# A two-layer decoder trunk on one core: Norm's matrix 64 bytes later, three short products, and eight more unread products at the start

## The chip, the core and the metric

The kernel runs on 1 core of one Trainium2 chip. A core has five engines, each with a queue of its own: TensorE (PE in the profile; its weight loads are listed apart as PEld and overlap the products), VectorE (DVE), ScalarE (ACT), GpSimd (POOL) and SyncE (SP, which issues DMAs here). DMAs move data between HBM and the on-chip memory. TensorE's results go to banks of a separate small memory, eight of 128 x 512 numbers here. The metric is the device time of one execution in microseconds (us). The time before is the median of 3 runs; the profile and the trace come from one more execution.

## What is computed

Two layers on a sequence of 512 tokens with 1024 features, float32. Each layer has a token mixer and a feed-forward part. Both get a root-mean-square norm of their input, scaled and shifted by values worked out from a vector `c`, and both are added to the residual stream through a gate. Cut to what matters:

```python
c_act = jax.nn.silu(c)
for i in range(2):
    mod = c_act @ ada_w[i] + ada_b[i]           # six vectors: shift, scale, gate, twice
    h = rmsnorm(x, norm_tok_g[i]) * (1.0 + sc_t) + sh_t
    y = retention_mixer(h, ...) if i == 0 else mlstm_mixer(h, ...)
    x = x + gt_t * y
    h = rmsnorm(x, norm_ffn_g[i]) * (1.0 + sc_f) + sh_f
    x = x + gt_f * conv_ffn(h, ...)
return rmsnorm(x, final_g)
```

`rmsnorm(x, g)` is `x * rsqrt(mean(x*x) + 1e-6) * g` over the features. Both mixers have four heads, with query and key projections of 256 columns and values and gates of 512 columns a head. Retention turns queries and keys by position (rope), the mLSTM sends them through a short causal convolution. The feed-forward part has 2 x 2816 inner features, a convolution over three tokens, and `silu(a) * b`.

## The kernel before, in words

**Arithmetic.** Every large product is made of three products of a faster format (float32r): a matrix is split into a high part `hi` and a low part `lo`, and `hi*hi + hi*lo + lo*hi` is summed (`mm3`). ScalarE makes high parts (`whi` for weights; `hh`, `t24h`, `t3h`, `yh`, `ggh` for activations), VectorE or ScalarE with an adding DMA the low ones (`wlo`, `hl` and so on). Activations lie with features on the 128 partitions and tokens along the row, so most products take a 128 x 128 weight block as the stationary matrix and 256 or 512 tokens as the moving one. Where the profile says "p<-hh,whi", the output bank is `p`, and `hh` and `whi` are what it reads.

**Folding.** Most projections are made in a Strassen-like scheme: two pairs of weight tiles (`wa`, `wb`) and sums of them (`ws`, `wt`) give seven products of 256 columns in place of eight. `seven` (line 824) lists the seven steps of one fold in the order 1, 2, 6, 5, 7, 4, 3 as items; `PairStream.product` (line 789 on) issues the twelve TensorE products of a step. A fold uses two banks, with the parts `c11`, `c12`, `c21`, `c22`. `c22` is first written by VectorE in the step for product 7. `fold_pairs` (line 853) makes two folds one after the other: for a head's query and key (`ret_q`, line 1754, `ml_q`, line 1896), or for its gates. The feed-forward part has 19 such folds a layer in `folded` (line 870), a unit of 84 products each, with the products that lead back to the residual stream ("po") among them.

**Stages.** In order of time: the opening with retention head 0 (`ret_start`, line 1604); retention heads 1 to 3, woven together by `heads` (line 1357): q, v and g are the projections, s the scores, a the attention, o the output projection; a boundary; the feed-forward part 0; a boundary; mLSTM heads 0 to 3, again by `heads`; a boundary; the feed-forward part 1; and the last boundary with the final norm. `heads` calls `q(2)` after head 0's output projection. mLSTM's `q(0)` comes after the value projection of `v_items` (line 1011), whose products have 512 columns.

**Boundaries.** `boundary` (line 1070) runs the last output blocks in two halves of the tokens ("po", 256 columns). In between, the norm's root for the first half is made: `SquareSum.root` (line 697) sums the squares over the partitions by two products "pms" with the matrix `ones_d`, filled with 1/1024, as stationary operand; the root for the second half is made in the same way during the first projection of the next part ("pf", `Start.rest`, line 1188). All weight tiles of a boundary and of its "pf" products start at column `OFF` = 16 (64 bytes) of their buffers, as do the folds' tiles. Plain projections ("pp", "po" with 512 columns) start at column 0. In the feed-forward part the class `Beside` (line 530) places the low part of every fourth block at 64 bytes off.

**Short products.** At the start of each boundary and of each feed-forward part's folds there is already a product of 16 columns ahead of the first real one (lines 913 and 1046). It reads the same weights and activations as the first product, and nobody reads its result:

```python
def short_product(o, w, b):
    PE.matmul(o, w, b, start=True, stop=True, skip_group_check=True)
```

**The opening.** `ret_start` adds up the squares of `x` on ScalarE and VectorE, makes the means over the partitions with `means` (line 1642: products "pms" that read one column of `ones_d` as the moving operand), the root, and a copy of it across partitions by four products with the identity `eye`. Meanwhile the modulation vectors come from VectorE's products with 512 KB tiles `ada`. Then eight rounds `products(k)` (line 1648) of 24 products each ("pst" and "pc") follow, each as soon as `h0[k]` is there (`hh` from ScalarE, `hl` from VectorE). Unread products keep TensorE at work in between: `busy(n)` (line 1616) issues n products of 512 columns of ones, 6, 1 and 1 times by the constant `BUSY`.

**Order.** All instructions are first collected by the class `Plan`, which keeps its own estimate of each one's time (`occ`) and due time, places them by due time on five queues with a model of buffers and transfers, and then issues them in that order; the order on each engine is fixed from there on. A product's estimated time feeds the due times of all that follows. On-chip buffers come from fixed pools: 62 slots of 512 columns, 18 wide tiles of 1024 + 64 columns (4352 bytes), and a pool of constants that is laid out one after the other, with `ones_d`, `ones_v` (1/512) and `ones_1` near its start:

```python
for name, v in (("d", 1.0 / D), ("v", 1.0 / DV), ("1", 1.0)):
    o = fixed(const, [P, P], F32R, f"ones_{name}")
    V.memset(o[:].bitcast(F32), v)
    ones[name] = o
```

Since every recorded instruction is issued by one helper, nearly all rows of the profile carry that helper's line, L386; groups are told apart by the tiles' names.

Of the kernel before, what the change touches and what calls it, by code (L numbers as in the profile page):

```python
# [16 lines left out]
P = 128  # L17
# [35 lines left out]
ROPE_DUE = 200.0  # L53
BUSY = (6, 1, 1)
ALIVE = (0, 0, 256, 256, 256, 256, 0, 0)
SUMMED = 6
# [333 lines left out]
def trunk(ctx: ExitStack, tc: tile.TileContext, xT, cb, pos, vec, ident, decay, zmask, ada, w_s0, w_in0, w_v0,  # L390
# [45 lines left out]
    for name, v in (("d", 1.0 / D), ("v", 1.0 / DV), ("1", 1.0)):  # L436
        o = fixed(const, [P, P], F32R, f"ones_{name}")
        V.memset(o[:].bitcast(F32), v)
        ones[name] = o
# [222 lines left out]
    def short_product(o, w, b):  # L662


        PE.matmul(o, w, b, start=True, stop=True, skip_group_check=True)

# [156 lines left out]

    def seven(use, streams, done, between=lambda j: None):

# [3 lines left out]
        def mk(n):  # L829
            def fn(w):  # L830
                if n == ORDER[0]:
                    for s in streams:
                        s.open(w[0])
                        fs.append(slot("fs"))
                for s, f in zip(streams, fs):
                    o = {1: s.c21, 2: s.c11, 5: s.c12, 3: s.c12}.get(n, s.c21)
# [15 lines left out]

    def fold_pairs(srcs, terms, thens, between=lambda j: None):

# [5 lines left out]
        for n, (src, then) in enumerate(zip(srcs, thens)):  # L860
            seven(FoldUse(src, n), [PairStream(terms, then)], each(then), lambda j: between(7 * n + j))

# [741 lines left out]
    def ret_start():  # L1604
# [10 lines left out]

        def busy(n, w=T):

            for _ in range(n):
                PE.matmul(pss[0][:, :w], ones["1"][:], warm[:, :w], start=True, stop=True, skip_group_check=True)

# [64 lines left out]
        for m in range(1, KT):  # L1685
            square(m)
            if m != SUMMED:
                add(m - 1, m)
            else:
                means(m - 1, True)  # L1690
            alive(m, ALIVE[m])
# [10 lines left out]
        gemv(0, 0, mod[0])  # L1702
        busy(BUSY[1])
        for t in range(4):
            PE.matmul(ps[:, t * P : t * P + P], rc[:, t : t + 1].broadcast_to([P, P]), eye[:, :P], start=True,
                      stop=True, skip_group_check=True)
        busy(BUSY[2])
        xr = xrs[0] = slot("xr")
# [45 lines left out]
    def ret_q(i, between=nothing):  # L1754
        thens = [half_pair(R[i], name, rope) for name in ("q", "k")]
        if i:
            fold_pairs(pair_srcs(w_in0, i * 8), sums0.terms, thens, between)
            return
# [304 lines left out]
```

## Time and profile before

| | |
|---|---|
| median of 3 runs | 1486.17 us (1485.03 to 1488.53) |
| the profiled execution's own time | 1483.02 us |
| its span | 1481.2 us |
| mean granted TensorE clock | 0.995 |
| TensorE busy | 1460.8 us (99%), 10550 products |
| VectorE busy | 1292.4 us (87%) |
| ScalarE busy | 1064.9 us (72%) |
| GpSimd busy | 267.1 us (18%) |
| DMA traffic | 306.16 MB, mean 207 GB/s |

The profile is one execution. The span goes from the first to the last instruction. A product's busy time in the profile is longer than the distance between two products, since they are pipelined: a product of 256 columns is listed with some 278 ns, while the next one starts some 115 ns later. So the pace of a stretch is read from starts: the stretch's length over the number of products that start in it. "Idle before, releaser" names the engine and tile whose end let an instruction start. The clock is the share of its full speed that TensorE was granted.

### The profile page before, as it was taken

How to read it: one execution, taken by the hardware profiler on the slowest of the kernel's cores; microseconds unless marked ns; L12 is line 12 of the kernel's file. 1: busy time of each engine (PE TensorE's matmuls, PEld its weight loads, DVE VectorE, ACT ScalarE, POOL GpSimd, SP SyncE). 2: the span in 40 equal slices, each digit the busy share in tenths (PEclk: the TensorE clock that was granted, in tenths of full speed). 3: DMA queues.
4: the chain of work that ended last, by engine and by line, in shares of the span. 5: the costliest groups of instructions: out<-in, count | busy, mean ns of one | idle time of the engine just before them, and what ended most of it. 6: DMA issues, size and time to landing. Idle time of an engine off the chain costs nothing. (4 is left out here: it accounts for less than half of the span.)

```text
span 1481.2 us, 27389 instructions
## 1 busy us (share of the span) xinstructions
PE 1460.8 (99%) x10550; PEld 1372.3 (93%) x10550; DVE 1292.4 (87%) x2167; ACT 1064.9 (72%) x1604; POOL 267.1 (18%) x295
## 2 busy tenths in 40 slices
PE   8999999999999999999999999999999999999998
PEld 6899999998999999999999998999989999999997
DVE  7899979787989889898897999999989988877866
ACT  5578758776588667676678985989856777667663
POOL 0334223222011111011001321222121011111010
PEclk8999999999999999999999999999999999999999
DMA  9878989887588999899567876878877678668661
GB/s 361 252 178 199 286 212 246 226 249 198 158 222 199 263 268 247 220 241 247 156 182 166 206 207 184 198 192 200 253 192 187 163 181 210 154 170 209 165 162 58
DMA packets 90821, 306.16 MB, mean 207 GB/s; under 512 B 11953, under 2 KB 14513, under 8 KB 90690
## 3 DMA queue, kind: packets, MB, share of 16 engines
q1 hardware_dynamic: 60882, 197.18, 38.8%
q0 software_dynamic: 29520, 106.97, 38.6%
q8 instruction: 82, 1.34, 0.4%
q14 instruction: 49, 0.40, 0.1%
q10 hardware_dynamic: 288, 0.27, 0.1%
HBM read 195.29 MB, written 2.12 MB: 133 GB/s over the span
## 5 line engine op out<-in xcount | busy, mean ns | idle before, releaser
L386 PE MATMUL p<-hh,whi 128*128 128x256 f32 x1026 | 284.3, 278 | 2.5 <-DVE p L386 2.5
L386 PE MATMUL p<-hl,whi 128*128 128x256 f32 x1024 | 283.5, 277 | 0.0
L386 PE MATMUL p<-hh,wlo 128*128 128x256 f32 x1024 | 281.2, 277 | 0.0
L386 ACT ACTIVATE wlo<-whi 128x1024 fp32r<-128x1024 f32 (+1 forms) x205 | 215.4, 1055 | 26.3 <-PE po L386 15.6
L386 PEld LDWEIGHTS p<-hh,whi 128*128 128x128 f32 x1026 | 193.0, 188 | 3.7 <-DVE p L386 3.1
L386 PEld LDWEIGHTS p<-hl,whi 128*128 128x128 f32 x1024 | 192.8, 188 | 0.5
L386 PEld LDWEIGHTS p<-hh,wlo 128*128 128x128 f32 x1024 | 191.3, 188 | 0.0
L386 PE MATMUL p<-t24h,whi 128*128 128x256 f32 x768 | 170.1, 278 | 3.3 <-DVE p L386 2.2
L386 PE MATMUL po<-ggl,whi 128*128 128x512 f32 (+1 forms) x448 | 152.8, 343 | 0.0
L386 PE MATMUL po<-ggh,whi 128*128 128x512 f32 (+1 forms) x448 | 151.9, 344 | 0.5 <-ACT whi L386 0.5
L386 PE MATMUL po<-ggh,wlo 128*128 128x512 f32 (+1 forms) x448 | 152.3, 343 | 0.0
L386 PE MATMUL p<-t24l,whi 128*128 128x256 f32 x512 | 142.0, 277 | 0.0
L386 DVE SCALAR_TENSOR_TENSOR x<-po,mod,x 128x512 f32<-128x512 f32 (+1 forms) x184 | 113.5, 628 | 30.6 <-PE po L386 29.8
L386 ACT CAST whi<-raw 128x1024 fp32r<-128x1024 f32 (+1 forms) x113 | 113.7, 1017 | 35.2 <-DMA raw<-w_s 9.2
L386 PEld LDWEIGHTS p<-t24h,whi 128*128 128x128 f32 x768 | 130.3, 188 | 5.8 <-DVE p L386 3.1
L386 DVE SCALAR_TENSOR_TENSOR cv<-p,vecs,cv 128x511 f32<-128x511 f32 (+1 forms) x152 | 111.2, 743 | 12.5 <-ACT cv L386 12.2
L386 DVE SCALAR_TENSOR_TENSOR ada<-ada,c_ext 128x1025 f32<-128x1025 f32 x96 | 119.6, 1247 | 0.6 <-DMA ada<-ada 0.6
L386 PE MATMUL po<-yl,whi 128*128 128x256 f32 (+1 forms) x352 | 115.6, 329 | 0.0
L386 PE MATMUL po<-yh,whi 128*128 128x256 f32 (+1 forms) x354 | 115.6, 329 | 0.0
L386 PE MATMUL po<-yh,wlo 128*128 128x256 f32 (+1 forms) x352 | 115.6, 329 | 0.0
L386 POOL DMA_DIRECT2D wlo<-wa x55 | 47.6, 866 | 353.6 <-ACT wlo L386 168.7
L386 ACT CAST whi<-ws 128x1024 fp32r<-128x1024 f32 x88 | 91.9, 1049 | 24.0 <-DVE ws L386 17.9
(292 smaller groups left out, 4418.9 us busy)
## 6 DMA issues: line engine op xcount, KB each, us to landing
ada<-ada SPq DMA_DIRECT2D x96, 512.5 KB, 6.6
wlo<-ws POOLq DMA_DIRECT2D x61, 512.0 KB, 7.2
wlo<-wa POOLq DMA_DIRECT2D x55, 512.0 KB, 6.5
wlo<-wt POOLq DMA_DIRECT2D x45, 512.0 KB, 6.5
wa<-w_up SPq DMA_DIRECT2D x38, 512.0 KB, 5.7
wb<-w_up SPq DMA_DIRECT2D x38, 512.0 KB, 7.9
wlo<-raw POOLq DMA_DIRECT2D x34, 512.0 KB, 8.0
raw<-w_o SPq DMA_DIRECT2D x32, 512.0 KB, 7.5
```

The lines of the kernel that those rows point to most:

```text
L386: getattr(c.obj, c.name)(*[real(v) for v in c.a], **{key: real(v) for key, v in c.k.items()})
```

## The change

Three things, and nothing else in the text of the kernel:

- `ones_d` starts 16 columns (64 bytes) into a buffer of 192 columns instead of at the start of one of 128.
- The first of the two folds of `ret_q(2)`, `ml_q(0)` and `ml_q(2)` gets a product of 16 columns ahead of its first one. It reads that product's weights and the first 16 columns of its activations and writes 16 columns of `c22`. Its planned time is zero.
- In `ret_start` eight more unread 512-column products are issued: four ahead of the means, one more ahead of the products with the identity, and three more behind them. Their planned time is zero too.

```diff
+EXTRA = (4, 1, 3)
...
-        o = fixed(const, [P, P], F32R, f"ones_{name}")
+        off = OFF if name == "d" else 0
+        o = fixed(const, [P, P + WPAD * (off > 0)], F32R, f"ones_{name}")[:, off : off + P]
         V.memset(o[:].bitcast(F32), v)
...
-    def seven(use, streams, done, between=lambda j: None):
+    def seven(use, streams, done, between=lambda j: None, lead=False):
...
+                    if lead:
+                        hi, hc, _, _ = w[0].p[n]
+                        short_product(streams[0].c22[:, :16], hi[:, hc : hc + P],
+                                      streams[0].terms(n, 0)[0][:, :16]).occ = 0.0
...
-    def fold_pairs(srcs, terms, thens, between=lambda j: None):
+    def fold_pairs(srcs, terms, thens, between=lambda j: None, lead=False):
...
-            seven(FoldUse(src, n), [PairStream(terms, then)], each(then), lambda j: between(7 * n + j))
+            seven(FoldUse(src, n), [PairStream(terms, then)], each(then), lambda j: between(7 * n + j),
+                  lead and not n)
...
-        def busy(n, w=T):
-            for _ in range(n):
-                PE.matmul(pss[0][:, :w], ones["1"][:], warm[:, :w], start=True, stop=True, skip_group_check=True)
+        def busy(n, w=T, free=0):
+            for i in range(n):
+                c = PE.matmul(pss[0][:, :w], ones["1"][:], warm[:, :w], start=True, stop=True, skip_group_check=True)
+                if i >= n - free:
+                    c.occ = 0.0
...
             else:
+                busy(EXTRA[0], free=EXTRA[0])
                 means(m - 1, True)
...
-        busy(BUSY[1])
+        busy(BUSY[1] + EXTRA[1], free=EXTRA[1])
...
-        busy(BUSY[2])
+        busy(BUSY[2] + EXTRA[2], free=EXTRA[2])
...
-            fold_pairs(pair_srcs(w_in0, i * 8), sums0.terms, thens, between)
+            fold_pairs(pair_srcs(w_in0, i * 8), sums0.terms, thens, between, i == 2)
...
-        fold_pairs(pair_srcs(w_in1, 1 + i * 8), start1.sums.terms, thens, between)
+        fold_pairs(pair_srcs(w_in1, 1 + i * 8), start1.sums.terms, thens, between, i in (0, 2))
```

More of the change, by code (lines that the diff above doesn't have):

```diff
@@ L662, in short_product @@
     def short_product(o, w, b):
-        PE.matmul(o, w, b, start=True, stop=True, skip_group_check=True)
+        return PE.matmul(o, w, b, start=True, stop=True, skip_group_check=True)
     def mm2(o, w, b, r=slice(None), start=True, stop=True):
```

## The prediction

> **What bounds the kernel now.** I read the page first.
>
> ```profile
> span 1481.2 us, 27389 instructions
> PE 1460.8 (99%) x10550; PEld 1372.3 (93%) x10550; DVE 1292.4 (87%) x2167; ACT 1064.9 (72%) x1604; POOL 267.1 (18%) x295
> ```
>
> TensorE is busy for 99% of the span, so what shortens its stream shortens the kernel, except where another engine hands it work late. The profiled execution took 1483.02 us: the span and 1.82 us around it. The median of the runs shown is 1486.17, 3.2 us more, so the sum is made against 1483.02 and its difference is carried to 1486.17. A measurement here tells about 0.2% (3.0 us) from no change.
>
> Next, the chain of waits (start, length, what), at its end: two halves of one stage, parted by Norm's two products.
>
> ```profile
> 1440.16 18.82 PE po L386 x166
> 1458.98 0.24 PE pms L386 x2
> 1459.21 12.74 PE po L386 x108
> ```
>
> Products of one shape run at two paces: 18.82 us / 166 = 113.4 ns each ahead of "pms", 12.74 / 108 = 118.0 after it. Then TensorE's busy time by stretch (start:end, length, busy, products touched, granted clock). In the first four rows and the last, two products of the count were already running at the left edge, in the others one.
>
> ```profile
> 373.28:392.30 19.02, 19.02 (x170) 1.00 0.43 136
> 392.30:429.16 36.86, 36.86 (x315) 1.00 0.72 172
> 734.14:769.95 35.81, 35.81 (x306) 1.00 0.60 173
> 1120.12:1156.75 36.63, 36.63 (x313) 1.00 0.69 173
> 194.26:211.22 16.96, 16.96 (x145) 1.00 0.73 209
> 797.18:828.15 30.97, 30.97 (x264) 1.00 0.97 242
> 923.24:942.21 18.97, 18.97 (x162) 1.00 0.78 195
> 1168.10:1171.70 3.60, 3.60 (x34) 1.00 0.87 175
> ```
>
> The second row starts just ahead of a boundary's first "pms", the next two likewise at two other boundaries. With these taken off: 19.02/168 = 113.2 ns ahead of "pms", then 36.86/313, 35.81/304 and 36.63/311 = 117.8 from it on; 16.96/144, 30.97/263 and 18.97/161 = 117.8 in the three groups of query tiles that the change opens with a short product; and 3.60/32 = 112.5 behind a short product that is there already. The granted clock is 1.00 in all of them. So there are two states of the weight and product stream, about 4.5 ns apart, and each lasts until something knocks the stream out of it.
>
> **Part 1: Norm's matrix.** Inside a boundary (the last two output blocks and the following projection) every weight tile starts OFF, 16 columns or 64 bytes, into its buffer; `ones_d` alone starts at 0. The stretch is fast up to the "pms" product and slow from it, in the boundary quoted on both sides and, by the chain, in the last. Put 64 bytes later, `ones_d` is in step with its neighbours, and I expect the pace before it to go on. That is 313 + 304 + 311 + 108 = 1036 products at 4.5 ns: **4.7 us**. That such an offset decides shows in the folded products of layer 0 too. They are broken by groups of twelve down products, whose weights start at 0 but for the last, a low part that `Beside` puts 64 bytes off. Here are the products behind a group that the planner cut after seven, and behind a full one:
>
> ```profile
> 467.92:469.10 1.18, 1.18 (x11) 1.00 1.08 271
> 485.33:486.69 1.36, 1.36 (x13) 1.00 1.07 286
> ```
>
> Less the one at the edge, 1.18/10 = 118 ns and 1.36/12 = 113. The stream is slow if the last weight ahead of it was not in step. `ones_d` also grows by 256 bytes, and every buffer behind it moves (rival 3). From below the price is zero (the pace has another cause), from above 1036 x (118.0 - 113.2) = 5.0. I take 4.7 because both sides of the step are on record in the same stage.
>
> The Trainium skill ("TensorE: Matmul & The Clock Gate", Part 2, step by step) says that TensorE has two independent read ports, and that loading the next weights takes no read bandwidth from the running matmul. By that rule a weight's address could not change the pace and this term would be 0, the sum 2.3; that is the first rival below. This trace has 113.2 and 117.8 ns for equal products at full clock, so I follow the trace.
>
> Do the boundaries keep it? The stalls behind boundaries one and three start from TensorE itself:
>
> ```profile
> 428.19 1.05 ACT L386 CAST whi<-wt 128x1024 fp32r<-128x1024 f32 x1 [2.92 <-PE pf L386]
> ```
> ```profile
> 1156.59 1.05 ACT wlo L386
> 1157.92 9.06 DMA wlo<-wt
> ```
>
> ```profile
> 445.64 0.39 PE L386 MATMUL p<-hh,whi 128*128 128x256 f32 x1 [1.19 <-DVE p L386]
> ```
>
> After the first boundary ScalarE had waited 2.92 us for the last "pf" product; from its casts a transfer and VectorE lead to TensorE's 1.19 us stall. After the third the chain has a low part made just then, and its 9.06 us transfer. Both start when "pf" ends, so its saving is passed on and the stalls keep their length. The second boundary has no stall behind it, and the fourth ends the kernel. The bound is VectorE, 87% busy: if it sets the pace of boundaries one and three, (313 + 311) x 4.5 = 2.8 us is lost.
>
> **Part 2: three short products.** What one costs and does is seen where the kernel has one (before the folded products), beside a group without:
>
> ```profile
> 1167.67 0.40 PE L386 MATMUL p<-hh,whi 128*128 128x16 f32 x2
> 1167.90 0.28 PE L386 MATMUL p<-hl,whi 128*128 128x256 f32 x1
> ```
> ```profile
> 797.19 0.28 PE L386 MATMUL p<-hh,whi 128*128 128x256 f32 x1
> 797.30 0.28 PE L386 MATMUL p<-hl,whi 128*128 128x256 f32 x1
> ```
>
> From 1167.67 to 1167.90 the short one and the first real product take 0.23 us, a first product alone 0.12: **0.11 us** each. It reads what the first product reads and writes a part of the bank that is overwritten later, so it adds no wait; its planned time is zero, so nothing else moves, and no DMA or queue is passed. Behind it the pace is 112.5. The gains:
>
> Retention head 2: slow from 194.26. But TensorE stalls at 216.07, and that comes from an earlier point:
>
> ```profile
> 205.83 0.37 ACT L386 COPY fs<-p 128x256 f32<-128x256 f32 x1 [3.92 <-PE p L386]
> ```
> ```profile
> 216.07 0.39 PE L386 MATMUL p<-t24h,whi 128*128 128x256 f32 x1 [1.60 <-DVE p L386]
> ```
>
> ScalarE waited for a product that ended at 205.8, then its queue and VectorE's ran full until 216. What is saved behind 205.8 only lengthens the stall. (205.8 - 194.3)/0.118 = 97 products x 4.5 = 0.44, less 0.11: **0.3**. mLSTM head 0: 263 x 4.5 = 1.18 less 0.11 = 1.07; VectorE waits for these products to the end, though for 0.34 and 0.18 us only:
>
> ```profile
> 828.48 0.43 DVE L386 TENSOR_TENSOR p<-p,fs 128x256 f32<-128x256 f32 x1 [0.34 <-PE p L386]
> 833.84 0.43 DVE L386 TENSOR_TENSOR p<-p,fs 128x256 f32<-128x256 f32 x1 [0.18 <-PE p L386]
> ```
>
> so I take **1.0** (bounds 0.34 + 0.18 - 0.11 = 0.4, and 1.07). mLSTM head 2: 161 x 4.5 - 0.11 = **0.6**; TensorE has no wait in its row. Together 1.9; if the pace stays slow, -0.33.
>
> **Part 3: eight products in the opening.** They fill TensorE's pauses before the first projection. The pauses and the clock:
>
> ```profile
> 13.09 1.95 PE L386 MATMUL pms<-ones_d,sq 128*128 128x1 f32 x16 [1.43 <-DVE sq L386]
> 16.34 2.08 PE L386 MATMUL pms<-eye,rc 128*128 128x128 f32 x8 [0.97 <-DVE rc L386]
> 20.19 2.07 PE L386 MATMUL pst<-whi,hh 128*128 128x512 f32 x4 [1.34 <-ACT hh L386]
> 28.30 1.07 PE L386 MATMUL pst<-whi,hh 128*128 128x512 f32 x4
> ```
> ```profile
> 12.00:15.40 3.40, 2.28 (x17) 1.97 (x17) 2.89 (x6) 0.53 (x1) 0.00 (x0) 1.00 1.02 417
> 15.40:18.80 3.40, 2.46 (x9) 2.00 (x9) 2.65 (x6) 0.80 (x3) 0.00 (x0) 0.50 1.03 421
> 18.80:22.20 3.40, 2.06 (x6) 1.63 (x6) 3.40 (x7) 2.20 (x4) 0.00 (x0) 0.50 1.02 416
> 22.20:25.66 3.46, 3.46 (x10) 2.69 (x9) 3.35 (x7) 1.77 (x2) 0.00 (x0) 0.50 1.03 416
> 25.66:28.30 2.64, 2.64 (x14) 2.16 (x13) 2.64 (x4) 1.06 (x1) 0.00 (x0) 1.00 1.02 418
> ```
>
> TensorE gets full clock at 12.0, loses it at 15.4 and has it again at 25.66. At half clock a 512-column product takes 3.46/8 = 0.43 us, at full clock 0.23:
>
> ```profile
> 50.05 1.07 PE L386 MATMUL pst<-whi,hh 128*128 128x512 f32 x4
> 50.96 0.39 PE L386 MATMUL pst<-hh,whi 128*128 128x512 f32 x1
> ```
>
> The four 512-column products from 50.05 take 0.91. The extras: four before the means, in 1.43 us of idle time (one at half and three at full clock, 1.1 us; at half clock throughout 1.7, so 0.3 late, which the wait of 0.97 us behind them covers); one in the 0.97; three in the 1.34, 0.7 at full and 1.3 at half clock, just fitting. So they delay nothing, or 0.1 at most. If they hold the clock, the 24 products from 20.19 to 28.30 take 5.4 us instead of 8.1: up to 2.7 saved; if not, nothing. But what follows isn't free to come earlier:
>
> ```profile
> 47.68 1.05 ACT L386 CAST whi<-raw 128x1024 fp32r<-128x1024 f32 x1 [1.74 <-DMA raw<-w_in]
> 48.63 0.72 ACT L386 ACTIVATE hh<-xr,mod 128x512 fp32r<-128x512 f32 x1
> ```
>
> The product at 50.05 needs the "hh" that ScalarE ended at 49.35, behind a cast that waited for a DMA: 0.7 us is all that TensorE can be early there, and the DMA engines are busy throughout (share 1.02 to 1.03 in the clock's rows). I take **0.4**, between 0 and 0.7.
>
> The Trainium skill (the same page, Part 1, the HAM clock gate) says that one busy window of about 3.4 us grants the full clock and one idle window takes it back. The trace agrees: its steps at 12.0, 15.4 and 25.66 lie 3.4 and 10.3 apart. By that rule the extras, which make the windows busy, could keep the clock from 12.0 on, this part would be 0.7, and the sum 7.3.
>
> **Sum**: 4.7 + 1.9 + 0.4 = 7.0 us. 1483.02 - 7.0 = 1476.0 for the profiled execution; 1486.17 - 7.0 = **1479.2** for the median.
>
> **Rivals.** (1) The matrix's place does nothing; "pms" breaks the stream because it is another stage's product. For it: no row shows `ones_d` elsewhere. Against it: the other weights there come from many buffers and break nothing. Then 7.0 - 4.7 = 2.3 us, 1483.9. (The Trainium skill's rule of two ports, above, would have it so.) (2) VectorE sets the pace of boundaries one and three: 7.0 - 2.8 = 4.2 us, 1482.0. For it its 87%; against it the 2.92 us for which ScalarE waited for "pf". (3) Slower: `ones_d` grows by 256 bytes, so every buffer behind it lies 256 bytes later. If the fast state hangs on addresses in steps of 512, the folded products flip: 2 layers x 19 units x 84 products x 4.5 ns = 14.4 us lost; 1486.2 - 2.3 + 14.4 = 1498.3. It decides from some 510 flipped products (2.3 us of other gain eaten), and is slower by 0.2% from 1180. Against it: neighbouring weight buffers are 4352 bytes apart, 17 x 256, so both cases occur already, and 19.02 us with 168 products from many buffers are all fast. (4) The change doesn't do what it says: the planner orders by due times, and a product of zero length could still alter a choice, or the unread products leave the state as it is; then between -2 and +3, about 1486.
>
> **Chances.** Forecast 0.68; (1) 0.11; (2) 0.13; (3) 0.03; (4) 0.05. The range goes from 1476.9 (the upper bounds, 5.0 + 2.0 + 0.7 = 7.7 us, give 1478.5; 1.6 is for the scatter of a median of runs that lay 1.1 below to 2.4 above theirs) to 1483.9, the first rival; it leaves out (3), most of (4) and the tails of the first two. Faster by over 0.2% (below 1483.2): nearly all of the forecast, three quarters of (2), a third of (1): 0.78. Slower: (3) and half of (4): 0.05. The same: 0.17.
>
> **What would show it.** Right: stretches behind "pms" at 113.3 ns a product, four times; the three query groups at 113; each stall behind them as long as now; full clock in 15.4 to 25.66, and a new wait of TensorE for "hh" near 50 us. Wrong: 117.8 behind "pms" (rival 1); the stall at 445, and the one behind the third boundary, longer by 1.4 each (2); 117.8 in the folded products (3); another order of instructions (4).

## The result and the profile after

The changed kernel took **1476.89 us** (median of 6 runs, 1474.96 to 1480.7), the kernel before 1485.78 in the same set (6 runs): a ratio of 0.994, interval 0.9926 to 0.9954, or 8.9 us. The forecast was 1479.2 and a range from 1476.9, so the time lies just below its low end. The profiled execution took 1476.27 us against 1483.02: 6.75 us, where the sum had said 7.0.

The head of the page of the changed kernel, and the end of its chain of waits (start, length, what):

```profile
span 1474.5 us, 27411 instructions
PE 1457.1 (99%) x10561; PEld 1367.3 (93%) x10561; DVE 1291.8 (88%) x2167; ACT 1064.2 (72%) x1604; POOL 267.9 (18%) x295
```
```profile
1433.91 18.81 PE po L387 x166
1452.72 0.23 PE pms L387 x2
1452.95 12.26 PE po L387 x108
```

TensorE carries 11 products more and is busy 3.7 us less. In the last boundary both sides of "pms" now run at the same pace: 18.81/166 = 113.3 ns a product ahead of it and 12.26/108 = 113.5 behind, where the kernel before had 118.0.

TensorE's busy time by stretch in the changed kernel (start:end, length, busy, products touched, granted clock, DMA share, GB/s):

```profile
371.67:407.37 35.70, 35.70 (x318) 1.00 0.57 146
407.94:427.02 19.08, 19.08 (x164) 1.00 0.75 185
731.10:765.85 34.75, 34.74 (x307) 1.00 0.62 177
1115.04:1150.40 35.36, 35.36 (x313) 1.00 0.71 179
193.30:209.52 16.22, 16.22 (x144) 1.00 0.77 218
793.27:823.00 29.73, 29.73 (x263) 1.00 1.00 248
918.42:934.55 16.13, 16.13 (x144) 1.00 0.77 200
```

315 products start in the first stretch, from the third of the boundary to Norm's second root: 113.3 ns each, straight across the first "pms" at 390.71. The second is what follows the second root in that boundary: 162 products at 117.8. The second and third boundaries, from their first "pms" on, are 34.75 and 35.36 us long, against 35.81 and 36.64 in the kernel before. Then come the three query groups behind their short products: 143, 262 and 142 products, 113.4 to 113.6 ns.

Where the first boundary falls back is seen in TensorE's timeline (start, length of the pipelined product, what, and in brackets the idle time before it and what ended it), which also shows three places that the prediction named:

```profile
48.76 1.20 PE L387 MATMUL pst<-whi,hh 128*128 128x512 f32 x4
...
214.49 0.39 PE L387 MATMUL p<-t24h,whi 128*128 128x256 f32 x1 [1.64 <-DVE p L387]
...
407.37 0.28 PE L387 MATMUL pms<-ssh,ones_d 128*128 128x256 f32 x1
407.61 0.39 PE L387 MATMUL pms<-ssl,ones_d 128*128 128x256 f32 x1
407.83 0.28 PE L387 MATMUL pf<-hh,whi 128*128 128x256 f32 x1
...
443.05 0.38 PE L387 MATMUL p<-hh,whi 128*128 128x256 f32 x1 [0.64 <-DVE p L387]
...
703.97 0.38 PE L387 MATMUL p<-t24h,wlo 128*128 128x256 f32 x1 [0.59 <-DMA wlo<-wt]
...
1166.87 0.38 PE L387 MATMUL p<-hh,whi 128*128 128x256 f32 x1 [1.18 <-DVE p L387]
```

The second "pms" product starts 0.24 us behind the first, not 0.11, and the next 0.22 behind that: TensorE now arrives before the low part of the squares ("ssl") is there. From there the pace is 117.8 again. The other two boundaries have such a pause too, at other places: starts 0.29 and 0.22 us apart some 50 products behind the second root's "pms" in the second boundary, and 0.20 apart some 30 products ahead of it in the third. Behind these the pace stayed at 113.3. At 48.76 there is no wait for "hh". The stall ahead of 214.49 is 1.64 us (1.60 before), the one ahead of 443.05 is 0.64 (1.19), and ahead of 703.97 stands a new one of 0.59 on a transfer of a low part.

Where the 6.75 us came from, by the start of the same instruction in both traces:

| point | before | after | lead |
|---|---|---|---|
| first plain projection | 66.38 | 65.22 | 1.2 |
| retention head 2, queries | 194.26 | 193.07 | 1.2 |
| their end | 211.22 | 209.52 | 1.7 |
| first boundary, "pms" | 392.30 | 390.71 | 1.6 |
| its end | 429.16 | 427.14 | 2.0 |
| second boundary, "pms" | 734.14 | 731.10 | 3.0 |
| mLSTM head 0, queries | 797.19 | 793.04 | 4.2 |
| their end | 828.15 | 823.00 | 5.2 |
| third boundary, "pms" | 1120.12 | 1115.04 | 5.1 |
| its end | 1156.75 | 1150.40 | 6.4 |
| last boundary, its first po after "pms" | 1459.21 | 1452.95 | 6.3 |
| end of the span | 1481.2 | 1474.5 | 6.7 |

The gains lie where the change was made: 1.2 in the opening, 0.43 + 1.06 + 1.28 + 0.49 = 3.3 in the boundaries, 0.51 + 1.02 + 0.48 = 2.0 in the query groups. The remaining 0.3 is the net of shorter and new stalls. These are two single executions; three more of the changed kernel follow below, and they differ. The clock in the opening of the changed kernel (columns as above, with the weight loads, VectorE, ScalarE and GpSimd behind TensorE):

```profile
12.42:15.83 3.41, 3.09 (x21) 2.22 (x19) 2.60 (x5) 0.83 (x1) 0.00 (x0) 1.00 1.00 408
15.83:19.24 3.41, 2.77 (x11) 2.57 (x12) 2.96 (x7) 0.82 (x3) 0.00 (x0) 0.50 1.03 418
19.24:22.66 3.42, 3.37 (x9) 2.16 (x8) 3.42 (x6) 1.95 (x5) 0.00 (x0) 0.50 1.03 419
22.66:26.06 3.40, 3.40 (x17) 2.80 (x16) 3.30 (x6) 1.71 (x2) 0.00 (x0) 1.00 1.03 418
```

The clock was lost at 15.83 all the same, and came back at 22.66, three microseconds sooner than in the kernel before.

### The profile page after: what moved, and what is told of

It reads as the page before. It is cut to its first block, busy times and chain, and to the rows that moved or that the text cites. A ratio compares the mean times of both kernels' runs of the same rounds, so it can differ in the third digit from the quotient of the medians.

```text
span 1474.5 us, 27411 instructions
## 1 busy us (share of the span) xinstructions
PE 1457.1 (99%) x10561; PEld 1367.3 (93%) x10561; DVE 1291.8 (88%) x2167; ACT 1064.2 (72%) x1604; POOL 267.9 (18%) x295
## 5 line engine op out<-in xcount | busy, mean ns | idle before, releaser
L387 PE MATMUL p<-hh,whi 128*128 128x256 f32 (+1 forms) x1029 | 284.2, 277 | 2.1 <-DVE p L387 2.0
L387 DVE SCALAR_TENSOR_TENSOR x<-po,mod,x 128x512 f32<-128x512 f32 (+1 forms) x184 | 113.4, 628 | 29.8 <-PE po L387 28.9
```

Source lines behind the costliest of these rows:

```text
L387: getattr(c.obj, c.name)(*[real(v) for v in c.a], **{key: real(v) for key, v in c.k.items()})
```

## The experiments

**Theory A**: the three parts add up, and what differs between sets of runs is the scatter of executions. **Theory B**: a part of the gain is missing from the sum, since 8.9 is more than 7.0. For the boundaries the rivals are that the place of `ones_d` does nothing, or that the move of all other buffers does it. Each set holds runs of the kernel before on the same chip; "before" in what follows is that set's own. Every kernel was profiled once.

### The kernel before, against itself

Nothing is edited but an empty line at the end.

> The kernel before, unchanged, so that its executions are listed with span and clock. Question: the change moved the median of the runs by 8.9 us, but the profiled execution by 6.75 only (1483.02 to 1476.27), because the profiled execution of before was 2.8 us faster than the median of the runs. Theory A (that one execution was a fast draw; runs scatter by the place where the clock's windows fall and by DMA waits): executions here between 1483 and 1488.5, median 1485.8, ratio 1.000, and the slower ones with a granted clock of 0.993 to 0.994 where the profiled one had 0.995. Theory B (profiled executions are faster than unprofiled ones): the profiled one again 2 to 3 us below all others.

1483.73 us (11 runs) against 1485.54 (29 runs): ratio 0.999, interval 0.9981 to 0.9999. The same code came out 1.5 us faster, with an interval that ends just short of no difference. The profiled execution took 1482.21, with a share of full clock of 0.993; runs at 0.999 took 1483.65 to 1486.58 and runs at 0.993 took 1482.21 to 1487.09, so the granted clock doesn't explain this scatter, though the two slowest of the 40, 1488.85 and 1490.19, are also the two at 0.992. The first theory of this run, with its median of 1485.8, missed by 2 us. The second, that profiled executions are faster, falls with the next run: the profiled execution of the eight products alone, 1484.49, lies above the median of its own runs. A gain of 1 or 2 us in one set proves nothing here.

### The parts alone

First the eight unread products on the kernel before, then Norm's matrix, then the three short products (with the lines of `seven` and `fold_pairs` that issue them).

```diff
+EXTRA = (4, 1, 3)
...
+                busy(EXTRA[0], free=EXTRA[0])
...
+        busy(BUSY[1] + EXTRA[1], free=EXTRA[1])
...
+        busy(BUSY[2] + EXTRA[2], free=EXTRA[2])
```

> The eight unread products alone. Step of the prediction: 0.4 us. The trace after shows TensorE 0.7 to 0.9 us ahead at 92 to 126 us, so theory A: 0.5 to 0.9 us faster, median 1485.0. Theory C (the clock's windows: in most executions before has the full clock later than in its profiled one, and the extras mend that): 2 to 3 us faster, median 1483, and the clock of all its runs at 0.995 or 0.996.

1482.38 (11 runs): ratio 0.9979, interval 0.997 to 0.9988, 3.1 us, about what theory C had given. Its clocks, 0.994 to 0.997, are not all at 0.995 or 0.996. In the trace the first plain projection starts at 65.25, 1.1 us sooner; no stretch after it is faster. TensorE in the timeline of this kernel:

```profile
48.79 1.20 PE L387 MATMUL pst<-whi,hh 128*128 128x512 f32 x4 [0.16 <-ACT hh L387]
```

Here the wait for "hh" that the prediction named is seen, with 0.16 us. The trace accounts for a third of the 3.1.

```diff
+        off = OFF if name == "d" else 0
+        o = fixed(const, [P, P + WPAD * (off > 0)], F32R, f"ones_{name}")[:, off : off + P]
```

> Norm's matrix alone. Forecast 4.7 us; the trace after shows the lead growing by 0.6, 0.9, 1.2 and 0.45 us inside the four boundaries, 3.2 in all, and shorter stalls behind the first (1.6 us in all), of which 0.8 is lost again at a stall at 703. Theory A: 3.2 to 4.7 us faster, median 1481 to 1482.5, products behind pms at 113.3 ns. Rival (1): no change and 117.8.

1481.09 (7 runs): ratio 0.9977, interval 0.9966 to 0.9989, 3.4 us. TensorE by stretch in this kernel, the first boundary from "pms" to its end:

```profile
391.75:427.45 35.70, 35.70 (x315) 1.00 0.74 178
```

35.70/313 = 114.1 ns over the whole of it, the pause at the second root included, and no product at 117.8: the same pause as in the changed kernel (0.23 and 0.22 us), but the stream came out of it fast. This execution, 1478.66, was the fastest of the seven. The four stretches are 35.70, 34.75, 35.36 and 12.47 us long: 1.17 + 1.06 + 1.28 + 0.49 = 4.0 us shorter than before. The query groups are as long as before.

```diff
-            fold_pairs(pair_srcs(w_in0, i * 8), sums0.terms, thens, between)
+            fold_pairs(pair_srcs(w_in0, i * 8), sums0.terms, thens, between, i == 2)
-        fold_pairs(pair_srcs(w_in1, 1 + i * 8), start1.sums.terms, thens, between)
+        fold_pairs(pair_srcs(w_in1, 1 + i * 8), start1.sums.terms, thens, between, i in (0, 2))
```

> The three short products alone. Forecast 1.9 us (0.3, 1.0 and 0.6); theory A: 1.5 to 2.2 us faster, median 1484. The three groups at 113.3 ns a product. If the parts add up to 7 and the whole gives 8.9, the parts help each other (a stall that goes when TensorE and its feeders shift).

1483.13 (11 runs): ratio 0.9984, interval 0.9974 to 0.9995, 2.4 us. The groups are 16.45, 29.95 and 16.36 us long against 16.96, 30.98 and 16.84: 0.5, 1.0 and 0.5, and the boundaries are as slow as before. Of the three parts the last two thus do what they should, in the stretch where they should. The medians of the parts add to 3.1 + 3.4 + 2.4 = 8.9, each with some 1.5 us of doubt. Against the 11 runs of the unedited kernel above (1483.73) they are 1.4, 2.6 and 0.6, which adds to 4.6: the medians of this set don't settle the sizes of the parts, the stretches in the traces do.

### All of it again, and without the opening

The changed kernel, with nothing edited.

> The changed kernel again, with more executions. The kernel before, unchanged, scattered by 8 us (1482.5 to 1490.2 in 29 runs and 1481.4 to 1486.5 in 11 more), with granted clocks of 0.993 to 0.999 that do not go with the time; so theory C is gone. Theory A (the parts add up, the rest of the 8.9 is scatter of the medians): 6 to 7.5 us faster than before, median 1478 to 1479. Theory B (the parts help each other): 8.5 to 9 us again, median 1476.5 to 1477.

1478.31 us (6 runs) against 1484.85 (26 runs): ratio 0.9958, interval 0.9943 to 0.9973, so 6.2 us. That is theory A's size. The trace shows what differs between executions of one kernel. TensorE by stretch: the second and the third boundary, each ahead of a point and behind it.

```profile
732.10:753.87 21.77, 21.76 (x192) 1.00 0.87 244
753.87:767.18 13.31, 13.31 (x116) 1.00 0.16 63
1116.71:1131.90 15.19, 15.19 (x137) 1.00 0.88 217
1132.10:1152.71 20.61, 20.61 (x177) 1.00 0.56 143
```

In the first execution of the changed kernel both boundaries were fast to their end. Here the stream fell back at the pause in each: 113 products at 117.8 behind it in the second boundary (second row) and 175 in the third (fourth row), though the starts at the pause stand as far apart as in the first execution: 0.28 and 0.23 us in the second boundary against 0.29 and 0.22, and 0.20 against 0.21 in the third. In the first boundary, where the pause is at the second root itself, both executions fell back.

Then the changed kernel less its lines with `EXTRA` and `free`:

```diff
-EXTRA = (4, 1, 3)
...
-                busy(EXTRA[0], free=EXTRA[0])
...
-        busy(BUSY[1] + EXTRA[1], free=EXTRA[1])
+        busy(BUSY[1])
...
-        busy(BUSY[2] + EXTRA[2], free=EXTRA[2])
+        busy(BUSY[2])
```

> The change without its eight opening products: matrix and short products stay. Theory A: 0.5 to 1.0 us slower than the changed kernel (the trace had 0.86 us of lead left at 92 us). Theory B: 2 us or more slower.

1480.63 (8 runs): ratio 0.9975, interval 0.9961 to 0.999, 3.7 us. That is 2.3 us above the changed kernel of the same set, where theory B had asked for 2 or more; the last set below comes back to it. The second boundary of this execution:

```profile
733.49:769.29 35.80, 35.80 (x306) 1.00 0.60 172
```

35.80/304 = 117.8: slow from beginning to end, with the matrix in its new place. The stream had already been slow ahead of "pms". So the new place doesn't make a stream fast; it lets a fast one go on.

### Which offset, and the other buffers

The kernel with the matrix alone, 128 bytes later in place of 64:

```diff
-        off = OFF if name == "d" else 0
+        off = 2 * OFF if name == "d" else 0
```

> Against the kernel before, Norm's matrix 128 bytes later instead of 64, in a buffer of the same 192 columns. If what counts is being in step with the neighbours, whose weights start 64 bytes into their buffers: as before, 117.8 ns behind every pms, no gain. If any other place would do (the old place met something): 113.3 ns and 3 to 4.5 us faster, as with 64.

1482.89 (11 runs): ratio 0.9987, interval 0.9979 to 0.9996. The first boundary, up to its second root and behind it:

```profile
391.81:408.51 16.70, 16.70 (x149) 1.00 0.70 159
408.96:428.16 19.20, 19.20 (x164) 1.00 0.74 186
```

At 128 bytes the matrix isn't in step with its neighbours, and yet the pace held up to the pause: the two products behind the first "pms" pair take 123 and 119 ns, and then it is 113 again. Behind the pause it is 117.8 (the second row has 163 starts), and the last boundary is slow from "pms" on (12.95 us). The four stretches are 36.46, 35.07, 35.51 and 12.95 us long, 2.3 us shorter than before where 64 bytes gave 4.0. In the second and the third boundary the second root's "pms" pair even met a stream at 117.8 and left it at 113.3. "In step or not" is too simple: an offset of 128 bytes disturbs, ends the fast pace in two of four places without a pause, and brings it back in two.

And the matrix at its old place in the larger buffer, so that only the buffers behind it move:

```diff
-        o = fixed(const, [P, P], F32R, f"ones_{name}")
+        o = fixed(const, [P, P + WPAD * (name == "d")], F32R, f"ones_{name}")[:, :P]
```

> Against the kernel before, the matrix stays at the start, but its buffer has 192 columns, so every buffer behind it lies 256 bytes later. Theory: nothing, 117.8 ns behind pms, 113.3 in the folded products, the time within 0.1% of before. Rival (3): folded products at 117.8, up to 14 us slower. If it were faster by 3 us or more, the move of the other buffers and not the matrix would have made the gain.

1484.71 (11 runs): ratio 1.0005, interval 0.9996 to 1.0014. The first two boundaries:

```profile
393.38:430.25 36.87, 36.87 (x316) 1.00 0.72 172
737.14:772.95 35.81, 35.81 (x307) 1.00 0.59 173
```

36.87 and 35.81, as before, to the hundredth. The move of the other buffers by 256 bytes does nothing, neither the gain nor the loss of the third rival. Over all traces, later ones included, with the matrix at 0 (seven) and at 64 bytes (seven; the two kernels of the next part are left out) the pattern has no exception: at 0 every "pms" pair that met a stream at 113.3 left it at 117.8 (25 of 25), and at 64 bytes every such pair without a pause left it at 113.3 (35 of 35).

### A third time, and more short products

The changed kernel, with nothing edited.

> The changed kernel once more, nothing altered; it settles which gain over the kernel before is the right one, since two sets of its runs gave -8.9 and -6.2 us. Theory A (the parts add up, 7.0 us, and what differs between sets is scatter): between 6 and 9 us under the kernel before of the same job, so that the mean of the three sets is 7 to 8. Rival (the first set's 8.9 is the true size and a part of the gain, some 2 us, was missed by the forecast): 8.5 to 9.5 here.

1478.51 (5 runs) against 1485.47 (15 runs): ratio 0.9949, interval 0.9935 to 0.9962, 7.6 us: theory A again.

Now a short product behind the second root, on the changed kernel:

```diff
+                if k0 == SPLIT:
+                    short_product(pss[0][:, 256:272], w[0].hi[:, k0 * P : k0 * P + P], h[k0].hi[:, :16]).occ = 0.0
                 for k in range(k0, k1):
```

> The changed kernel with one more short product of 16 columns in each of three boundaries, ahead of the products that follow Norm's second root; it reads the first such product's weights. Theory: the stall of about 0.23 us at Norm's two products throws the stream back to 117.8 ns in some executions (162 products in the first boundary of the changed kernel's first profile, 114 and 176 in the second and third boundary of its second), and a short product behind the stall brings it to 113.3 again. Then all three boundaries show over 300 products at 113.3 in the profile, and the time is 0 to 1.4 us under the changed kernel (162 x 4.5 = 0.73 us gained in a boundary that was thrown back, 3 x 0.11 paid). Rival (what broke the stream is the weights of Norm's matrix at their new place after all, or the part that follows is held by VectorE): 117.8 stays behind the stall and the time is 0.3 us above.

The added product of this kernel and the next starts a sum (`start=True`) in a bank whose other half is still being summed, and both kernels compute another result than the kernel before; they serve to time the stream and are no kernels to use. 1478.53 (5 runs): ratio 0.995, interval 0.9938 to 0.9963, the same as the changed kernel beside it (1478.51). TensorE behind the short product of the first boundary, then ahead of that of the third and behind it:

```profile
408.57:426.81 18.24, 18.24 (x163) 1.00 0.77 190
1116.70:1135.64 18.94, 18.94 (x168) 1.00 0.89 249
1135.99:1152.71 16.72, 16.72 (x143) 1.00 0.49 96
```

In the first boundary it did what was expected: 161 products at 113.3 in place of 162 at 117.8. In the third the stream had come out of the pause fast (113 ns for the 27 products before), and the short product itself threw it back: 142 at 117.8. In the second the stream was slow before it and behind it. One gain, one loss.

Then a short product ahead of every fold, values and gates included, on top of those three:

```diff
-                  lead and not n)
+                  lead)
...
-            fold_pairs(pair_srcs(w_in0, i * 8), sums0.terms, thens, between, i == 2)
+            fold_pairs(pair_srcs(w_in0, i * 8), sums0.terms, thens, between, True)
...
-        fold_pairs(pair_srcs(w_in1, 5 + i * 8), start1.sums.terms, [ml_gate(i)] * 2)
+        fold_pairs(pair_srcs(w_in1, 5 + i * 8), start1.sums.terms, [ml_gate(i)] * 2, lead=True)
```

> The changed kernel with the short product ahead of every fold of the mixers (29 more, values and gates included) and with the three of the run before. In the changed kernel's profile some 1160 products of the heads still run at 117.8, in runs of 70 to 160. If a short product always brings the pace to 113.3, up to 1160 x 4.5 = 5.2 us would come back, 32 x 0.11 = 3.5 us is paid where nothing is gained: between 1.7 us faster than the changed kernel and, if the stalls by other engines take the gain, 3.5 us slower. I take 0: the change's three places were those where a long slow group started without other products woven in.

1487.29 us (11 runs): ratio 1.001, interval 1.0001 to 1.0019; 8.8 us above the changed kernel, far past what was expected. A part of that is not the products: with 32 more of them, though planned at zero, the plan put some 270 products in other places, and the time isn't clean. The trace is worth more. Six stretches, in pairs parted by a short product between their edges:

```profile
144.94:151.89 6.95, 6.95 (x60) 1.00 1.00 230
152.48:158.71 6.23, 6.23 (x57) 1.00 1.01 273
194.37:200.83 6.46, 6.46 (x59) 1.00 0.85 258
201.06:206.48 5.42, 5.42 (x47) 1.00 1.02 232
800.73:807.19 6.46, 6.46 (x60) 1.00 0.96 199
807.41:817.19 9.78, 9.78 (x84) 1.00 0.92 244
```

With 59, 55, 57, 46, 57 and 83 products started in them: 117.8 then 113.3; 113.3 then 117.8; 113.3 then 117.8. The trace has 39 short products in all. Eight come behind a run of 48 or more products of 512 columns, and the stream is at 113 behind all eight; three of these places are the change's own, where the kernel before, without a short product, ran at 117.8. Five come behind only one or two products of 512 columns, and behind four of them it runs at 118. Eleven come into a stream of 256 columns that ran at 113: behind ten it runs at 118 (in one of them for some seven products only), and behind one other waits follow at once. Of fifteen in a stream at 118 five brought it to 113, nine didn't, and behind one other waits follow. A short product doesn't set the fast pace. It disturbs; behind a long run of 512 columns it leaves the fast pace every time, and in a fast stream it ends it in all ten cases that can be read.

### The opening, taken apart

Two sets put 3.1 us (the eight alone) and 2.3 us (the changed kernel with and without them) on the eight products, where the trace has 1.2. The 3.8 of the expectations below compares runs of different sets.

The kernel with the eight products alone, cut to the last three:

```diff
-EXTRA = (4, 1, 3)
+EXTRA = (0, 0, 3)
```

> The kernel before with only the three unread products behind the identity, EXTRA = (0, 0, 3). Theory: of the eight these three are the ones that work. In the trace of before the window 18.80 to 22.20 had TensorE at work for 2.06 us of 3.40 and the full clock came only at 25.66; in the changed kernel the window 19.24 to 22.66 has 3.37 of 3.42 and the full clock comes at 22.66. Then here too: full clock about 3.4 us sooner than 25.66, the first plain projection (66.38 in before, 65.22 after) near 65.2, and the time 0.9 to 1.3 us under the kernel before, if the whole of it is kept. Rival (the four ahead of the means matter as much, or the opening is worth about 3 us as two sets of runs would have it: 7.5 with it and 3.7 without, and 3.1 alone): the first plain projection stays near 66.3 here, or the time is 2.5 to 3.5 us under.

1485.72 (12 runs) against 1484.42 (23 runs): ratio 1.0006, interval 0.9997 to 1.0015. No gain. The clock in two stretches of the opening, and TensorE's timeline there:

```profile
17.40:20.90 3.50, 3.50 (x12) 3.10 (x13) 3.47 (x7) 1.98 (x4) 0.00 (x0) 1.00 1.03 420
20.90:24.30 3.40, 3.40 (x16) 2.81 (x15) 3.40 (x5) 1.50 (x2) 0.00 (x0) 1.00 1.02 412
```
```profile
19.06 2.00 PE L387 MATMUL pst<-warm,ones 128*128 128x512 f32 x4
20.90 1.09 PE L387 MATMUL pst<-whi,hh 128*128 128x512 f32 x4
21.83 0.39 PE L387 MATMUL pst<-hh,whi 128*128 128x512 f32 x1
```

The clock column says 1.00 in both stretches, but the products say otherwise: the four from 19.06 take 1.84 us to the next start, 0.46 each, and the four from 20.90 take 0.93, 0.23 each. The column stands at 1.00 until the first step that the trace records, whatever the products do; here that step is at 20.87. So TensorE had the full clock from 20.9, 4.8 us sooner than in the kernel before, and the first plain projection starts at 64.86. In the trace the theory came true, in the time it didn't.

At 25.8 TensorE was 1.9 us ahead of the kernel before, though 1.0 behind at 18. Its timeline shows where that went:

```profile
90.23 0.39 PE L387 MATMUL p<-t24h,whi 128*128 128x256 f32 x1 [0.63 <-ACT fs L387]
...
92.43 0.38 PE L387 MATMUL p<-hh,whi 128*128 128x256 f32 x1 [0.55 <-DVE p L387]
```

Two waits that the kernel before doesn't have there, 0.63 for ScalarE's copy and 0.55 for VectorE's sum, and at 92.4 the lead of 1.5 was gone. What was saved in the opening was lost in the first fold here. In the first trace of the changed kernel 0.8 of its 1.15 was left at this point.

And cut to the first five:

```diff
-EXTRA = (4, 1, 3)
+EXTRA = (4, 1, 0)
```

> The kernel before with only the four unread products ahead of the means and the one ahead of the identity, EXTRA = (4, 1, 0). Theory: the clock is lost near 15.4 to 15.8 all the same, since TensorE's idle time ahead of the identity remains, and comes back only near 25.7, since the pause of 1.34 us ahead of the first projection remains; the first plain projection near 66.4 and no gain (0, within 0.5 us either way). Rival (the first five hold the clock or bring the root sooner): full clock before 25, the first plain projection below 65.8, a gain of 1 us and more.

1485.1 (12 runs): ratio 1.0002, interval 0.9993 to 1.001. No gain, as the theory had it, but the trace is as the rival had it: full clock again from 23.3, and the first plain projection at 65.47.

Then without the eight products, as above, and the changed kernel with nothing edited, in the same set.

> Norm's matrix and the three short products without the eight unread ones, once more; beside the changed kernel in the same set. Theory A (the opening's part is what the trace shows, 0.9 to 1.3 us, and the 3.8 us between the two in other sets is the scatter of medians of 5 to 11 runs): 0 to 2 us above the changed kernel of this set. Rival (the opening is worth some 3 us, in a way that single traces don't show): 3 us or more above it.

> The changed kernel once more, nothing altered, to stand beside the run without the eight unread products. Theory A: 6 to 9 us under the kernel before (7.0 from the sum; the three sets so far gave 8.9, 6.2 and 7.6 by their ratios), and 0 to 2 us under the run without them. Rival: 3 us or more under it.

The changed kernel without the eight products: 1478.56 (5 runs), ratio 0.9954, interval 0.9942 to 0.9966. The changed kernel: 1477.49 (6 runs), ratio 0.9952, interval 0.994 to 0.9963. So the eight products are worth 1.1 us or less in this set: theory A. The 2.3 of the earlier set, with medians of 6 and 8 runs, is scatter by that. None of the kernels tried is faster than the changed one. The clock of the execution without them:

```profile
18.30:21.70 3.40, 2.71 (x10) 2.01 (x9) 3.37 (x8) 2.42 (x4) 0.00 (x0) 1.00 1.03 418
21.70:25.10 3.40, 3.40 (x10) 2.63 (x9) 3.29 (x7) 1.05 (x1) 0.00 (x0) 1.00 1.03 417
```

Here too the 1.00 is not the products' pace: the second stretch touches 10 products of 512 columns where a stretch at full clock touches 16 or 17, and the first step that the trace records, to the full clock, is at 26.24. Read with this, the traces agree with each other. In the seven with all eight products the full clock is back between 18.4 and 23.7 us and the first plain projection starts at 65.22 to 65.44. In the eight without any it is back between 23.8 and 26.4 us, in one at 20.0, and that projection starts at 64.89 to 66.91, on average at 66.08. The eight products thus save some 0.8 us up to that point, and steady it.

The four traces of the changed kernel also tell how much of Part 1 lasts. At the pauses the stream fell back in the first boundary in all four, in the second in one, in the third in three. The boundaries together are 3.3, 2.0, 2.5 and 2.5 us shorter than in the kernel before. In the three traces of kernels with the matrix in its new place and without the eight products, the first boundary stayed fast; why is not shown.

## Why the prediction was right or wrong, point by point

**The step that failed** is the last one: "1.6 is for the scatter of a median of runs that lay 1.1 below to 2.4 above theirs", and with it the carrying of the sum to a median of three runs. Over all sets, 99 runs of the kernel before have a median of 1485.03 us (1481.7 to 1490.19) and 23 of the changed kernel 1477.52 (1474.37 to 1482.29): 7.5 us. The miss of 1479.2 - 1476.89 = 2.3 us is then 1.1 from the base (1486.17 in place of 1485.03), 0.5 from the sum (7.0 in place of 7.5) and 0.6 because the first six runs lay below the median of all. The range took 1.6 for the median of runs of the new kernel and nothing for the base, whose three runs have a scatter of the same size. The four sets gave 8.9, 6.2, 7.6 and 7.1 us by their ratios.

That the sum of 7.0 came so near is in part luck. Part 1 was too large by 1.4 to 2.7 (3.3, 2.5, 2.5 and 2.0 in the four traces, for 4.7), Part 3 too small by 0.4 to 0.8, and what changes outside the three parts was put at nothing. On average the traces account for 2.6 + 2.0 + 0.8 = 5.4 of the 7.5 us; where the other 2 come from stays open. The 6.75 of the profiled execution is a draw as well: the other three profiled executions of the changed kernel were 2.9 to 3.4 us faster than the same one of the kernel before. Some 0.8 of that difference lies behind the stall near 1170, where some 170 more products ran at 117.8 in these three, and also in the second execution of the kernel before.

**Part 1, Norm's matrix (forecast 4.7): right in its mechanism, too large.** The matrix alone made all four stretches fast, and the move of the other buffers did nothing: the first and the third rival are out. In the profiled execution it gave 3.3, at best (matrix alone) 4.0. Two things were not in the working: the pauses of some 0.2 us, one in each of the first three boundaries, which the profile of the kernel before does not have (in the first TensorE now comes before the squares' low part); and that the stream can fall back at such a pause, by execution in one boundary or another. Rule and row: the Trainium skill ("TensorE: Matmul & The Clock Gate", Part 2, step by step) has two independent read ports; taken as the prediction took it, the 64 bytes could change nothing. The four stretches of 36.87, 35.81, 36.64 and 12.96 us with the matrix at 0, and 35.70, 34.75, 35.36 and 12.47 with it 64 bytes later, speak against it.

**VectorE as the bound of boundaries one and three (rival 2): out.** Their gains were kept: the lead grew from 1.6 to 2.0 and from 5.1 to 6.4, and at the next boundary it was 3.0 and 6.3. In the other three traces 0.9 to 1.1 us was lost on the way to the last boundary, but mostly to products at 117.8 and not to a wait. The stalls behind them were to stay as long as they were. The one ahead of 443.05 became shorter instead, 0.64 for 1.19, and in another execution 0.46; the one ahead of 1166.87 is 1.18, where the kernel before has 1.05, and 1.24 to 1.44 in the other three traces.

**Part 2, three short products (1.9): right, 2.0.** By groups 0.5, 1.0 and 0.5 against 0.3, 1.0 and 0.6. The stall at 214.49 hardly grew (1.64 for 1.60), so what was saved behind 205.8 was kept after all. The reason given, that the short product brings the fast pace, is too broad: it held in places behind long runs of products of 512 columns (96, 120 and 100 of them), and not behind one or two of them or in a fast stream.

**Part 3, eight products (0.4): small, as forecast, and for another reason.** The clock wasn't kept from 15.4; it came back 3.0 us sooner. That gave 1.2 in the profiled execution, more than the bound of 0.7, because "hh" was not fixed: ScalarE's cast and "hh" ahead of 48.76 came sooner too,

```profile
47.04 1.05 ACT L387 CAST whi<-raw 128x1024 fp32r<-128x1024 f32 x1 [2.43 <-DMA raw<-w_in]
47.99 0.72 ACT L387 ACTIVATE hh<-xr,mod 128x512 fp32r<-128x512 f32 x1
```

47.99 against 48.63, since the transfer before the cast landed sooner; why it did is not shown. Over all traces the clock came back sooner with the eight products, and the first plain projection started 0.8 us sooner on average. In the medians the part is worth between nothing (three products, five products) and 3.1 (the eight alone), and 1.1 or less in the last set. The Trainium skill ("TensorE: Matmul & The Clock Gate", Part 1, the HAM clock gate) has windows of about 3.4 us; the clock's steps in the traces agree, 6.8 us apart in the changed kernel and 10.2 in the kernel before, two and three windows. The trace doesn't bear out the prediction's case that the extras make every window busy enough: the clock was lost behind a stretch with 3.09 us of work in 3.41.

**The plan (rival 4): out.** The eleven products are in, and no other instruction of TensorE, VectorE or ScalarE has another place.

## What to carry to other kernels

Where equal products run at two paces, look for what stands at the seam: a stationary matrix at another offset than its neighbours can end the fast pace for hundreds of products, and a fix is worth no more than the next pause leaves of it. A short product in front helped where it followed a long run of products of another width; put into a stream that is already fast, it costs what it was meant to bring. A gain of less than half a per cent needs several sets of runs on both sides: here one and the same kernel differed by 1.5 us between two loads, and a forecast for a median of a few runs has to allow for the scatter of the base as well as that of the result.

## What the runs showed that was not expected

- The pace of products of 256 columns has two values, 113.3 and 117.8 ns at full clock, and the stream can fall from the first to the second at a pause of about 0.2 us, though not in every execution.
- With Norm's matrix 128 bytes off the first boundary ran at 113 up to its second root, and the last at 117.7; 64 bytes gave 113.3 to 113.5 in both.
- TensorE's clock was lost behind a stretch with 3.09 us of work in 3.41 (12.42 to 15.83 in the changed kernel) and kept through one with 2.71 in 3.41, in the changed kernel's fourth trace:

```profile
18.52:21.93 3.41, 2.71 (x12) 1.84 (x11) 3.41 (x6) 2.33 (x4) 0.00 (x0) 1.00 1.03 418
```

  Busy time by the profile doesn't settle it, and where the windows fall differs between executions.
- The clock column reads 1.00 ahead of the first recorded step of a trace, also where products of 512 columns start 0.43 us apart, as at half clock. It is to be read together with the products' pace.
- What scatters between executions of one kernel is the stream's pace and a handful of stalls on transfers: 0.64 and 0.46 us ahead of the same product near 443 in two executions of the changed kernel, and 0.59 or nothing ahead of the one near 704. What throws the pace one way or the other at a pause stays open.
